# A hybrid attention block: where the attention's blocks are turned, and what stands in line ahead of what in the gates and at SwiGLU's end

## The chip, the cores and the metric

The kernel runs on one core of a Trainium2 chip. Its five engines (TensorE or PE for matmuls, VectorE or DVE, ScalarE or ACT, GpSimd or POOL, and SyncE or SP, which here only issues transfers) each work through a queue of their own in order and wait for one another by semaphores. The metric is the device time of one execution in microseconds (us), as a median of runs.

## What is computed

One residual layer over 512 tokens and 16 learned meta tokens of width 1024. Both attentions, their projections, the gates and SwiGLU are computed in fp32 to full precision; cut to what matters:

```python
xn = rmsnorm(h, norm_mix_g)
proj = xn @ w_in                                  # sq, sk, sv of 8 heads; dq, dk (two maps each), dv of 8 heads
# A: stick-breaking, blocks of 128 queries
z = q @ k.T * 128 ** -0.5                         # kpos < qpos
u = log_sigmoid(-z)
a = exp(log_sigmoid(z) + reverse_cumsum(u) - u)
o_sb = a @ v
# B: differential
p = softmax(q_c @ k_c.T / 8 - slope * dist)       # c = 0, 1; whole chunks of 64 ahead are seen
o_df = (p[0] - lam * p[1]) @ v                    # then a norm per head
gates = sigmoid(xn @ w_gate + b_gate)             # 2 x 1024
merged = gates[0] * (o_sb @ w_br_sb) + gates[1] * (o_df @ w_br_df)
h = h + merged @ w_out
hn = rmsnorm(h, norm_ffn_g)
h = h + (silu(hn @ w_ffn_gate) * (hn @ w_ffn_up)) @ w_ffn_down
y = rmsnorm(h, norm_final_g)[meta dropped]
```

## The kernel before

**Products.** Every fp32 product is made of three matmuls on numbers cut into a high part (`h`) and a rest (`l`): `mm3` (L291) issues high x high (L294), high x rest (L295) and rest x high (L296). The cut of a tile is two instructions in `split` (L77): ACT copies the high part (L78), DVE subtracts it for the rest (L79). Weights pass in chunks of 512 KB through SP's queue (L208) into `wst`, and `generic` (L220) splits each into `wh` and `wl` a few chunks ahead of its use.

**Order.** A planner orders each engine's queue at build time from program order, dependences, priorities (`tc.high_priority(offset=EVAC)` pulls evacuations forward) and its own model of time. So an instruction can stand in a queue ahead of one that comes before it in the program. `behind(ins, name)` (L81) adds a dependence on an instruction kept in `cast`, so that `ins` comes after it.

**Attention.** Eight stick-breaking heads (`sb_head`, L614), then eight differential ones (`df_head`, L698). While a head's scores are made into probabilities by ACT and DVE, PE runs projections of the next head and other "units" in the places where the head's generator yields a number (L1038). `attn_out` (L548) turns a head's probabilities so that PE can multiply them with v: ten blocks of 128 x 128, by PE transposes (L559, L561) into PSUM. Row j = 0 of blocks has four, j = 1 three, j = 2 two, and one diagonal block is kept plain. `turn_first` turns j = 0 and 1 (seven blocks) into two banks, each followed by its evacuation into `a_h` (ACT, L563) and `a_l` (DVE, L564), and makes the small edge blocks `a_s` by DVE's own transposes (L572). One unit of PE work later `turn_rest` turns the other three and copies `a_f` (ACT, L578). One more unit later `weighted` (L580) multiplies: three groups of `mm3`, then `a_f` and `a_s` (L586, L587).

PSUM has eight banks: two `z` tiles of two banks each (`z_tile`) and four `mm` tiles of one bank (`mm_tile`; `tr_tile` is the same pool). The stick-breaking head turns j = 0 and 1 into the first banks of two `z` tiles and the other three blocks into the second bank of the first of them. The differential head uses three `mm` tiles. `weighted` takes a `z` tile in both.

**Gates.** The loop over `merge_order` (L1115) goes through the eight column blocks f in the order 1, 2, 0, 3, ... 7. For both branches it loads y from DRAM (SP, L1069), takes the gate (from the unit, or for f = 0 from DRAM, L1121) and multiplies: on POOL for f < 6 (L1127), on DVE for 6 and 7 (L1129). DVE adds the two (L1133), for f = 3 to 6 behind the last weight split. `merge_sums` splits the result for the output product. Loads of x into `hres` on POOL's queue are placed behind the last POOL product (L1142).

**SwiGLU.** Gate and up products are made in seven products a block pair (a Strassen-like scheme in 256-token halves): `first`, `second`, `third` for each of the 22 column blocks f. In `second` (L1321) ACT copies `qx` out of bank e1 after product s2, so that s3 can write there, and `qy` after s3; DVE adds e3 to `qy`. In `third` (L1335) product a22 goes to e1 and makes `aT[:, f, T1]`, then s4 goes to e3 and makes `aT[:, f, T2]` by a silu. For f = 21, the last, no `first(f + 1)` stands between `second` and `third`. The down products follow; `act_parts` (L1366) splits their activations (`da`: ACT L1374, DVE L1375), and the planner may place those and the first down weights early.

Of the kernel before, what the change touches and what calls it, by code (L numbers as in the profile page):

```python
# [9 lines left out]
F32 = mybir.dt.float32  # L10
# [31 lines left out]
def block_kernel(ctx: ExitStack, tc: tile.TileContext, x, meta, norm_mix_g, w_in, w_gate, b_gate,  # L42
# [33 lines left out]

    def split(hi, lo, src, lo_eng=None, hi_copy=None):  # L77
        cast["last"] = (hi_copy or nc.scalar.copy)(hi, src)  # L78
        cast["lo"] = (lo_eng or nc.vector).tensor_tensor(lo, src, hi.bitcast(F32), op=ALU.subtract)  # L79

# [139 lines left out]
    def generic(n):  # L220
        wh, wl = parts(n)
        split(wh, wl, staged[n], nc.gpsimd if n < 3 else None)
        cast["split"] = cast["lo"]
# [323 lines left out]

    def attn_out(blocks, d, lo_rows, banks):  # L548

# [5 lines left out]

        def turn(j, pt):
            n = 512 - j * P
            for t in range(j, NQ):
                nc.tensor.transpose(pt[:, (t - j) * P:(t - j + 1) * P], blocks(t, j * P, (j + 1) * P), ident)  # L559
            if j == 2:  # L560
                nc.tensor.transpose(pt[:, 384:512], blocks(3, 3 * P, 4 * P), ident)  # L561
            c = slice(off[j], off[j] + n)
            nc.scalar.copy(a_h[:, c], pt[:, 0:n])  # L563
            nc.vector.tensor_tensor(a_l[:, c], pt[:, 0:n], a_h[:, c].bitcast(F32), op=ALU.subtract)  # L564

        def turn_first():
            for j, pt in enumerate(banks(2)):
                turn(j, pt)
            for t in range(NQ):
                b = blocks(t, (t + 1) * P - 32 + NM, (t + 1) * P + NM)  # L570
                for i in range(qn // 32):
                    nc.vector.transpose(a_s[32 * t:32 * t + 32, t * qn + 32 * i:t * qn + 32 * i + 32],  # L572
                                        b[lo_rows + 32 * i:lo_rows + 32 * i + 32])

        def turn_rest():
            p2 = banks(1)[0]
            turn(2, p2)
            nc.scalar.copy(a_f, p2[:, 384:512])  # L578

# [10 lines left out]

        return turn_first, turn_rest, weighted

# [21 lines left out]
    def sb_head(h, d, o_h, o_l):  # L614
# [29 lines left out]
        base = ((0, 0), (0, 144), (0, 416), (1, 0))  # L644
        zs = []

        def banks(n):
            if n == 1:
                return [zs[0][:, 1]]
            zs.extend((z_tile(), z_tile()))  # L650
            return [z[:, 0] for z in zs]

        t1, t2, av = attn_out(lambda t, k0, k1: res[base[t][0]][:, base[t][1] + k0:base[t][1] + k1], d, 96, banks)
        yield 4 if h + 1 < SEVEN else 5
        t1()
        yield 1
        t2()
        yield 1
        ps = av()
# [38 lines left out]
    def df_head(h, d, o_h, o_l):  # L698
# [55 lines left out]
        maps(3)  # L754
        t1, t2, av = attn_out(lambda t, k0, k1: prs[t][:, 0, k0:k1], d, 64, lambda n: [tr_tile() for _ in range(n)])
        yield 3 if h < NH - 1 else 2
        t1()
        yield 1
        t2()
        yield 1  # L760
        ps = av()
# [353 lines left out]
    for i, f in enumerate(merge_order):  # L1115
# [3 lines left out]
        for br, y in enumerate(ys[i]):  # L1119
            if f == 0:  # L1120
                nc.sync.dma_start(sg[br], g_part[br])  # L1121
                nc.scalar.activation(sg[br], sg[br], AF.Sigmoid)
            elif f > 2:
                for u in gate(br, f, sg[br], AF.Sigmoid):
                    u()
            if f < 6:
                cast["gated"] = nc.gpsimd.tensor_tensor(sg[br], sg[br], y, op=ALU.mult)  # L1127
            else:
                nc.vector.tensor_tensor(sg[br], sg[br], y, op=ALU.mult)  # L1129
        if f == KT - 1:  # L1130
            prepare(prep_at["out", "s1", 2])
        m = mf[:, f] if f < 4 else sg[0]
        merged = nc.vector.tensor_tensor(m, sg[0], sg[1], op=ALU.add)  # L1133
        if 2 < f < KT - 1:
            behind(merged, "split")
# [144 lines left out]
    with tc.tile_pool(name="ffn", bufs=1) as fp:  # L1280
# [40 lines left out]
        def second(f):  # L1321
# [3 lines left out]
            with tc.high_priority(offset=EVAC):  # L1325
                nc.scalar.copy(qx, e1)  # L1326
            ready(at_job(c3, f) + 2)
            product(f, "s1", tsum["t1"], e3, True)
            product(f, "s3", tsum["t3"], e1, False)
            with tc.high_priority(offset=EVAC):  # L1330
                nc.scalar.copy(qy, e1)
                nc.vector.tensor_tensor(qy, e3, qy, op=ALU.add)
            return qx, qy

        def third(f, qx, qy):  # L1335
            e1, e2, e3, sg = bank[f]
            product(f, "a22", tsum["t4"], e1, False)
            with tc.high_priority(offset=EVAC):
                nc.vector.scalar_tensor_tensor(aT[:, f, T1], e1, -1.0, sg[:, T1], op0=ALU.mult, op1=ALU.mult)
            product(f, "s4", tsum["b22"], e3, False)  # L1340
            with tc.high_priority(offset=EVAC):
                nc.vector.tensor_tensor(sg[:, T2], e3, qx, op=ALU.add)
            nc.scalar.activation(sg[:, T2], sg[:, T2], AF.Silu)
            nc.vector.scalar_tensor_tensor(aT[:, f, T2], qy, -1.0, sg[:, T2], op0=ALU.mult, op1=ALU.mult)

# [20 lines left out]
        def act_parts(upto):  # L1366

            for i in range(len(acts), min(len(order_of), upto)):
# [4 lines left out]
                src, sign = block(b, k0), -1.0 if b == "t2" else 1.0  # L1373
                nc.scalar.activation(a[:, 0, 0:n], src, AF.Copy, scale=sign)  # L1374
                nc.vector.scalar_tensor_tensor(a[:, 1, 0:n], src, sign, a[:, 0, 0:n].bitcast(F32), op0=ALU.mult, op1=ALU.subtract)  # L1375
# [163 lines left out]
```

## Time and profile before

| what | value |
|---|---|
| median of 3 runs | 944.86 us (944.44 to 946.46) |
| the profiled execution | 942.7 us |
| its span, first to last instruction | 940.9 us |
| PE busy | 925.6 us |
| DVE busy | 731.7 us |
| ACT busy | 582.3 us |
| POOL busy | 188.2 us |

The span is what the engines' records cover; the rest of the execution's time lies around it. A busy PE is not a PE at its peak: matmuls are pipelined, a record of 0.39 us is followed by the next one's start 0.23 us later, so the distance of the starts tells what a matmul costs, and a wait costs its idle time and some of the overlap. The views used are: the page; the waits (who waited for whom, in total, times, longest); windows (busy time and count of each engine in a stretch, then clock, DMA share, GB/s); and the timeline (start, duration, engine, line, operation, output<-inputs, shape, count, and in brackets the idle time before it and what ended it). Stages by the timeline: stick-breaking heads to about 225 us, differential heads to 490, gates to 560, output product and norm to 610, SwiGLU to 829, down product to the end.

### The profile page before, as it was taken

To read this page: it belongs to the slowest core of one execution; us is meant where nothing else is said; L and a number is where in the kernel's file an instruction comes from. 1 tells how busy PE (TensorE), PEld (TensorE's weight loads), DVE (VectorE), ACT (ScalarE), POOL (GpSimd) and SP (SyncE) were. 2 spreads that over 40 slices of the span, in tenths; PEclk is the share of its full clock that TensorE was granted. 3 is DMA by queue.
4 is the path that set the end of the run, shared out by engine and by line. 5 is a ranking of instruction groups with operands and counts; after the bars stand their busy time and mean duration, and the time that the engine had idled before them with its cause. 6 is when DMAs were issued, how large, how long until landed. Compare 5 with 4: busy or idle time off the path is not lost.

```text
span 940.9 us, 16049 instructions
## 1 busy us (share of the span) xinstructions
PE 925.6 (98%) x6010; PEld 842.0 (89%) x6010; DVE 731.7 (78%) x1400; ACT 582.3 (62%) x1102; POOL 188.2 (20%) x211
## 2 busy tenths in 40 slices
PE   8999999999999999999999999999999999999997
PEld 5988999898999899998988788899999999988886
DVE  7988877776677766877662678899888888999775
ACT  7665676676656666666754456765555555566554
POOL 4000121222333344343504440001000000000013
PEclk9999999999999999999999999999999999999999
DMA  8525778778777878799977775627753343286642
GB/s 250 152 62 157 174 175 198 166 168 250 190 194 175 219 173 190 172 194 200 195 184 190 191 260 165 168 73 165 156 131 105 101 125 90 68 267 202 198 150 90
DMA packets 155823, 158.41 MB, mean 168 GB/s; under 512 B 6465, under 2 KB 117218, under 8 KB 155746
## 3 DMA queue, kind: packets, MB, share of 16 engines
q1 hardware_dynamic: 132690, 101.61, 36.2%
q0 software_dynamic: 22896, 55.72, 28.7%
q8 instruction: 47, 0.77, 0.3%
q14 instruction: 30, 0.25, 0.1%
q10 hardware_dynamic: 160, 0.07, 0.0%
HBM read 133.64 MB, written 50.86 MB: 196 GB/s over the span
## 4 chain that ended last, share of the span: by engine, by line
PE 79%; DVE 11%; issue 3%; ACT 3%; DMA 1%; POOL 1%; SPq 0%; ACTq 0%; POOLq 0%; DVEq 0%
PE mm L295 18%; PE mm L296 18%; PE mm L294 18%; PE z L294 6%; PE z L296 6%; PE z L295 6%; DVE wl L79 3%; DVE s L640 2%; PE z L709 1%; PE z L708 1%; PE tr L559 1%; DVE s L641 1%; DVE s L636 1%; PE tr L535 1%; POOL y_df L804 1%
## 5 line engine op out<-in xcount | busy, mean ns | idle before, releaser
L295 PE MATMUL mm<-xT_l,wh 128*128 128x264 f32 (+2 forms) x656 | 213.6, 326 | 0.5
L294 PE MATMUL mm<-xT_h,wh 128*128 128x264 f32 (+2 forms) x656 | 213.6, 326 | 0.5 <-ACT xT_h L913 0.5
L296 PE MATMUL mm<-xT_h,wl 128*128 128x264 f32 (+2 forms) x656 | 212.7, 324 | 0.5 <-DVE wl L79 0.5
L79 DVE TENSOR_TENSOR wl<-wst,wh 128x1024 fp32r<-128x1024 f32 (+1 forms) x147 | 165.8, 1132 | 32.6 <-ACT wh L78 32.2
L78 ACT CAST wh<-wst 128x1024 fp32r<-128x1024 f32 (+1 forms) x147 | 141.8, 966 | 77.0 <-PE mm L295 56.2
L296 PEld LDWEIGHTS mm<-xT_h,wl 128*128 128x128 f32 x656 | 123.5, 188 | 10.9 <-DVE wl L79 0.9
L295 PEld LDWEIGHTS mm<-xT_l,wh 128*128 128x128 f32 x656 | 123.4, 188 | 10.3 <-DVE xT_l L914 1.3
L294 PEld LDWEIGHTS mm<-xT_h,wh 128*128 128x128 f32 x656 | 123.4, 188 | 9.9 <-ACT xT_h L913 0.9
L294 PE MATMUL mm<-hT_h,wh 128*128 128x256 f32 x304 | 85.8, 284 | 1.4 <-ACT qx L1326 0.8
L296 PE MATMUL mm<-hT_h,wl 128*128 128x256 f32 x304 | 85.9, 283 | 0.0
L295 PE MATMUL mm<-hT_l,wh 128*128 128x256 f32 x304 | 85.7, 283 | 0.0
L294 PEld LDWEIGHTS mm<-hT_h,wh 128*128 128x128 f32 x304 | 57.9, 191 | 2.0 <-ACT qx L1326 1.3
L296 PEld LDWEIGHTS mm<-hT_h,wl 128*128 128x128 f32 x304 | 58.0, 191 | 0.0
L295 PEld LDWEIGHTS mm<-hT_l,wh 128*128 128x128 f32 x304 | 58.0, 191 | 0.0
L712 DVE CUSTOM_DVE_ANT_0 pr<-z,bias 128x144 f32<-128x144 f32 (+3 forms) x64 | 30.9, 501 | 34.2 <-PE z L709 31.9
L294 PE MATMUL mm<-o_h,wh 128*128 128x512 f32 x128 | 53.0, 414 | 0.0
L1441 POOL TENSOR_TENSOR outs<-hres,gF 128x512 f32<-128x512 f32 x4 | 6.2, 1546 | 222.7 <-DVE hres L1427 216.0
L294 PE MATMUL z<-wh,da 128*128 128x512 f32 (+1 forms) x132 | 50.2, 381 | 0.0
L295 PE MATMUL z<-wl,da 128*128 128x512 f32 (+1 forms) x132 | 50.2, 381 | 0.0
L296 PE MATMUL z<-wh,da 128*128 128x512 f32 (+1 forms) x132 | 50.2, 380 | 0.0
L296 PE MATMUL mm<-o_h,wl 128*128 128x512 f32 x128 | 50.1, 391 | 0.0
L295 PE MATMUL mm<-o_l,wh 128*128 128x512 f32 x128 | 50.0, 390 | 0.0
(364 smaller groups left out, 2507.7 us busy)
## 6 DMA issues: line engine op xcount, KB each, us to landing
wst<-in_w_in_dram SPq DMA_DIRECT2D x40, 512.0 KB, 6.1
ds<-in_w_ffn_down_dram POOLq DMA_DIRECT2D x30, 512.0 KB, 6.0
wst<-in_w_ffn_gate_dram SPq DMA_DIRECT2D x22, 512.0 KB, 3.9
wsu<-in_w_ffn_up_dram SPq DMA_DIRECT2D x20, 512.0 KB, 4.0
wst<-in_w_gate_dram SPq DMA_DIRECT2D x16, 512.0 KB, 6.4
y_df<-y_out POOLq DMA_DIRECT2D x32, 256.0 KB, 7.8
slots<-ds SPq DMA_DIRECT2D x13, 512.0 KB, 3.3
os<-in_w_out_dram POOLq DMA_DIRECT2D x12, 512.0 KB, 4.6
```

Source lines behind the costliest of these rows:

```text
L78: cast["last"] = (hi_copy or nc.scalar.copy)(hi, src)
L79: cast["lo"] = (lo_eng or nc.vector).tensor_tensor(lo, src, hi.bitcast(F32), op=ALU.subtract)
L294: nc.tensor.matmul(ps, lhsT=ah, rhs=bh, start=(start and i == 0), stop=False, skip_group_check=skip)
L295: nc.tensor.matmul(ps, lhsT=ah, rhs=bl, start=False, stop=False, skip_group_check=skip)
L296: nc.tensor.matmul(ps, lhsT=al, rhs=bh, start=False, stop=(stop and i == n - 1), skip_group_check=skip)
L535: nc.tensor.transpose(pt[:, j * P:(j + 1) * P], vT[:, j * P:(j + 1) * P], ident)
L559: nc.tensor.transpose(pt[:, (t - j) * P:(t - j + 1) * P], blocks(t, j * P, (j + 1) * P), ident)
L636: nc.vector.scalar_tensor_tensor(s, zz, 0.0, e, op0=ALU.max, op1=ALU.add)
L640: nc.vector.tensor_tensor_scan(f, resets[:, L - (b - a):][:, ::-1], f, BIG, op0=ALU.mult, op1=ALU.add)
L641: nc.vector.tensor_tensor(s, zz, s, op=ALU.subtract)
L708: nc.tensor.matmul(o, lhsT=q[c][:, qs], rhs=k[c][:, 0, k0:k1], start=True, stop=False)
L712: nc.vector.tensor_tensor_reduce(po, zz, bb, scale=1.0, scalar=-3.0e38, op0=ALU.add, op1=ALU.max, accum_out=mx[:, t, c:c + 1])
```

## The change

Three edits. First, `attn_out` turns all ten blocks in one place, before any of their copies, into the four banks of two `z` tiles in both kinds of head (j = 0 and j = 2 in the banks of the first, j = 1 and the diagonal block in those of the second); the copies follow, then the edge blocks; two units then stand between this place and `weighted`. Second, the gate products of f < 6 go from POOL to DVE, and the merge of f = 0 also goes behind the last weight split. Third, at SwiGLU's end the first down weight's high part is cast behind `qy` of the last block, the first two activation parts behind its `qx`, and the last block's `third` makes its s4 half before its a22 half.

```diff
-    def split(hi, lo, src, lo_eng=None, hi_copy=None):
+    def split(hi, lo, src, lo_eng=None, hi_copy=None, after=None):
         cast["last"] = (hi_copy or nc.scalar.copy)(hi, src)
+        if after:
+            behind(cast["last"], after)
...
-        split(wh, wl, staged[n], nc.gpsimd if n < 3 else None)
+        split(wh, wl, staged[n], nc.gpsimd if n < 3 else None, after="qy" if n == first_down else None)
...
-        def turn(j, pt):
...
-        def turn_first():
...
+        def turned():
+            z0, z1 = z_tile(), z_tile()
+            banks = z0[:, 0], z1[:, 0], z0[:, 1]
+            for j, pt in enumerate(banks):
+                for t in range(j, NQ):
+                    nc.tensor.transpose(pt[:, (t - j) * P:(t - j + 1) * P], blocks(t, j * P, (j + 1) * P), ident)
+            nc.tensor.transpose(z1[:, 1, 0:P], blocks(3, 3 * P, 4 * P), ident)
+            for j, pt in enumerate(banks):
+                n = 512 - j * P
+                c = slice(off[j], off[j] + n)
+                nc.scalar.copy(a_h[:, c], pt[:, 0:n])
+                nc.vector.tensor_tensor(a_l[:, c], pt[:, 0:n], a_h[:, c].bitcast(F32), op=ALU.subtract)
+            nc.scalar.copy(a_f, z1[:, 1, 0:P])
             for t in range(NQ):
...
-        def turn_rest():
-            p2 = banks(1)[0]
-            turn(2, p2)
-            nc.scalar.copy(a_f, p2[:, 384:512])
...
-        t1()
-        yield 1
-        t2()
-        yield 1
+        turned()
+        yield 2
...
+            gated = nc.vector.tensor_tensor(sg[br], sg[br], y, op=ALU.mult)
             if f < 6:
-                cast["gated"] = nc.gpsimd.tensor_tensor(sg[br], sg[br], y, op=ALU.mult)
-            else:
-                nc.vector.tensor_tensor(sg[br], sg[br], y, op=ALU.mult)
+                cast["gated"] = gated
...
-        if 2 < f < KT - 1:
+        if f not in (1, 2, KT - 1):
             behind(merged, "split")
...
-                nc.scalar.copy(qx, e1)
+                cast["qx"] = nc.scalar.copy(qx, e1)
...
-                nc.scalar.copy(qy, e1)
+                cast["qy"] = nc.scalar.copy(qy, e1)
...
+            for half in (up, gate_and_up) if f < NFF - 1 else (gate_and_up, up):
+                half()
...
-                nc.scalar.activation(a[:, 0, 0:n], src, AF.Copy, scale=sign)
+                part_h = nc.scalar.activation(a[:, 0, 0:n], src, AF.Copy, scale=sign)
+                if i < 2:
+                    behind(part_h, "qx")
```

`up` holds the a22 half and `gate_and_up` the s4 half of `third`, each with its evacuations as before.

More of the change, by code (lines that the diff above doesn't have):

```diff
@@ L546, in v_units, with attn_out @@
         return kv_units(key, lambda ps, s: nc.scalar.copy(vT[:, s], ps)), turn
-    def attn_out(blocks, d, lo_rows, banks):
+    def attn_out(blocks, d, lo_rows):
         qn = P - lo_rows
@@ L554, in attn_out @@
         a_f = ap_.tile([P, P], F32, tag="a_f", name="a_f")
-        def turn(j, pt):
[L557 to L564, printed above, removed]
-        def turn_first():
-            for j, pt in enumerate(banks(2)):
-                turn(j, pt)
+        def turned():
[11 more added lines that the diff above has]
+            nc.scalar.copy(a_f, z1[:, 1, 0:P])
             for t in range(NQ):
@@ L589, in weighted @@
             return ps
-        return turn_first, turn_rest, weighted
+        return turned, weighted
     def sb_units(h):
@@ L644, in sb_head @@
         base = ((0, 0), (0, 144), (0, 416), (1, 0))
[L645 to L653, printed above, removed]
+        turned, av = attn_out(lambda t, k0, k1: res[base[t][0]][:, base[t][1] + k0:base[t][1] + k1], d, 96)
         yield 4 if h + 1 < SEVEN else 5
-        t1()
-        yield 1
-        t2()
-        yield 1
+        turned()
+        yield 2
         ps = av()
@@ L754, in df_head @@
         maps(3)
-        t1, t2, av = attn_out(lambda t, k0, k1: prs[t][:, 0, k0:k1], d, 64, lambda n: [tr_tile() for _ in range(n)])
+        turned, av = attn_out(lambda t, k0, k1: prs[t][:, 0, k0:k1], d, 64)
         yield 3 if h < NH - 1 else 2
[L757 to L760, printed above, removed]
+        turned()
+        yield 2
         ps = av()
@@ L1336, in third, with up, gate_and_up @@
             e1, e2, e3, sg = bank[f]
[L1337 to L1344, printed above, removed]
+            def up():
+                product(f, "a22", tsum["t4"], e1, False)
+                with tc.high_priority(offset=EVAC):
+                    nc.vector.scalar_tensor_tensor(aT[:, f, T1], e1, -1.0, sg[:, T1], op0=ALU.mult, op1=ALU.mult)
+            def gate_and_up():
+                product(f, "s4", tsum["b22"], e3, False)
+                with tc.high_priority(offset=EVAC):
+                    nc.vector.tensor_tensor(sg[:, T2], e3, qx, op=ALU.add)
+                nc.scalar.activation(sg[:, T2], sg[:, T2], AF.Silu)
+                nc.vector.scalar_tensor_tensor(aT[:, f, T2], qy, -1.0, sg[:, T2], op0=ALU.mult, op1=ALU.mult)
+            for half in (up, gate_and_up) if f < NFF - 1 else (gate_and_up, up):
+                half()
         for f in range(2):
```

## The prediction

> **What bounds the kernel now.** I read the page first, then PE's waits, then short windows around each stall, then the timeline of those places.
>
> ```profile
> span 940.9 us, 16049 instructions
> ...
> PE 925.6 (98%) x6010; PEld 842.0 (89%) x6010; DVE 731.7 (78%) x1400; ACT 582.3 (62%) x1102; POOL 188.2 (20%) x211
> ```
>
> TensorE is the bound: 15.3 us of the span are not PE. No edit here removes a matmul or a transposed block, so all that can be won is PE's idle time and what a restart costs. The longest wait by cause, and the windows around the first six stick-breaking heads:
>
> ```profile
> PE z L559 <- DVE a_l L564: 1.8, 2, 1.0
> ...
> 48.00:57.00 9.00, 8.01 (x67) 7.75 (x66) 8.89 (x18) 4.46 (x10) 0.00 (x0) 1.00 0.01 2
> 79.00:87.00 8.00, 7.88 (x52) 6.98 (x51) 7.93 (x15) 5.46 (x10) 1.30 (x2) 1.00 0.71 205
> ...
> 161.00:170.00 9.00, 8.17 (x53) 7.29 (x52) 8.90 (x17) 6.78 (x12) 1.69 (x3) 1.00 0.69 196
> 188.00:197.00 9.00, 8.89 (x56) 7.84 (x55) 8.91 (x17) 6.62 (x12) 2.28 (x3) 1.00 0.76 220
> ```
>
> First column behind the window: its length, then PE's busy time. PE is idle 0.99 us in the first, 0.83 in the fifth, and about 0.12 in the other four (the first and the last of them are shown): 2.3 together. DVE is nearly full in each (8.89 of 9.00). So in these heads PE waits for a DVE that is behind.
>
> **Part 1, the ten blocks.** Now the blocks of a head are turned as 7 and, one unit of matmuls later, 3. The late three go into the second bank of the tile whose first bank is still being read:
>
> ```profile
> 82.76 1.15 DVE L564 TENSOR_TENSOR a_l<-z,a_h 128x512 fp32r<-128x512 f32 x2
> ...
> 83.49 0.44 PE L559 MATMUL z<-ident,s 128*128 128x128 f32 x2
> ...
> 85.63 0.42 DVE L564 TENSOR_TENSOR a_l<-z,a_h 128x256 fp32r<-128x256 f32 x1
> ...
> 86.62 0.40 PE L294 MATMUL z<-a_h,vh 128*128 128x512 f32 x1
> ```
>
> The first a_l of the pair ends at about 83.37 (0.6 us of the 1.15), and the late blocks start 0.12 behind it. After the change the three are issued before any copy reads the tiles, so this wait cannot be there. What it costs is more than the idle time, as a head with the wait and one without it show:
>
> ```profile
> 188.92 0.93 PE L559 MATMUL z<-ident,s 128*128 128x128 f32 x7
> ...
> 195.99 0.40 PE L294 MATMUL z<-a_h,vh 128*128 128x512 f32 x1
> ...
> 216.07 0.93 PE L559 MATMUL z<-ident,s 128*128 128x128 f32 x7
> ...
> 222.84 0.40 PE L294 MATMUL z<-a_h,vh 128*128 128x512 f32 x1
> ...
> 224.85 0.60 PE L535 MATMUL tr<-ident,vT 128*128 128x128 f32 x4
> ...
> 225.28 0.27 PE L542 MATMUL tr<-ident,v_s 128*128 128x128 f32 x1
> ```
>
> From the first block to the weighted sum: 7.07 us with the wait, 6.77 without, for the same work; 0.30 for 0.11 idle, so a restart costs about 0.19. Over six heads: 2.3 + 6 x 0.19 = 3.4 us lost. A block itself takes 0.11 (four in 0.43), in one group or in two: moving three is free.
>
> What is late next? The weighted sum needs the third a_l, now 85.63 to 86.05. It goes to right behind the pair, about 84.3, with PE wanting it at 86.3: two us of room. Head 0 has less:
>
> ```profile
> 54.75 0.55 DVE L564 TENSOR_TENSOR a_l<-z,a_h 128x384 fp32r<-128x384 f32 x1
> ...
> 56.70 0.40 PE L294 MATMUL z<-a_h,vh 128*128 128x512 f32 x1
> ```
>
> Without the 1.15 us of its stall PE gets there at 55.55, while the second a_l ends at 55.30 and the third at about 55.7; up to 0.3 of the stall may remain. DVE's and ACT's work queued behind (weight halves, kl, vT) moves back by the third copy, 0.4 us, and no wait for those shows in these windows. I take **2.9 of the 3.4 us**; bounds 0 (DVE's lateness turns up at the next wait) and 3.4.
>
> In the eight differential heads the blocks move from mm tiles to z tiles:
>
> ```profile
> 276.14 0.93 PE L559 MATMUL tr<-ident,pr 128*128 128x128 f32 x7
> ...
> 278.55 1.16 DVE L564 TENSOR_TENSOR a_l<-tr,a_h 128x512 fp32r<-128x512 f32 x2
> ...
> 280.44 0.48 PE L294 MATMUL z<-a_h,vh 128*128 128x512 f32 x1
> ```
>
> There is no idle time to win. There is a new wait: the weighted sum's own z tile is one of the two just used, so it starts only when the copies out of that one are done. The pair of a_l ends at 279.71; the third (0.42) would end near 280.1, 0.3 before PE's 280.44. I take **nothing**; bounds 0 and the rival below.
>
> The clock is 1.00 in every window above, those with seven blocks in a row among them, so ten should not change it. The Trainium skill (TensorE: Matmul & The Clock Gate, Part 4: PE-mode transpose) says that transposes do not count as PE activity in the way matmuls do, which speaks against longer runs of them. By that rule the granted clock could fall behind each group; the windows do not bear it out, and it is a rival below.
>
> **Part 2, the gates.** Twelve gate products go from POOL to DVE, and the merge of f=0 is queued behind the last weight split.
>
> ```profile
> 527.35 1.30 POOL L1127 TENSOR_TENSOR sg<-sg,y_df 128x512 f32<-128x512 f32 x1 [0.71 <-ACT sg L1122]
> ...
> 528.68 0.69 DVE L1133 TENSOR_TENSOR mf<-sg 128x512 f32<-128x512 f32 x1 [1.76 <-POOL sg L1127]
> 529.29 2.31 DVE L79 TENSOR_TENSOR wl<-wst,wh 128x1024 fp32r<-128x1024 f32 x1
> ...
> 530.55 0.39 PE L294 MATMUL mm<-xT_h,wh 128*128 128x512 f32 x1
> 530.78 0.39 PE L295 MATMUL mm<-xT_l,wh 128*128 128x512 f32 x1
> 531.66 0.50 PE L296 MATMUL mm<-xT_h,wl 128*128 128x512 f32 x1 [0.49 <-DVE wl L79]
> ...
> 559.16 0.69 DVE L1129 TENSOR_TENSOR sg<-sg,y_sb 128x512 f32<-128x512 f32 x1
> ```
>
> DVE stood at f=0's merge 1.76 us for POOL's product; the weight half behind it, 2.31 us where the same form takes 1.22 (826.16 below), came too late. PE steps 0.88 there where its step is 0.23 (530.55 to 530.78), and I add 0.11 for the restart, the smaller of those seen here: 0.76 lost. After the change the half goes first and a product costs DVE 0.69 in place of POOL's 1.30. The twelve add 12 x 0.69 = 8.3 us to a DVE that stands waiting in this stage; the products of f=6 and 7 are already done so. In the other queues: SP's loads of the next y stand behind the products and come 0.6 earlier each; POOL's last three y_df accumulations are no longer behind a waiting product; the hres loads start earlier. I take **0.75**; bounds 0.76 and a loss where a product waiting for its y holds up weight halves behind it (a rival).
>
> **Part 3, the end of SwiGLU.** In f=21 ACT's copy qx comes behind the first down weight's cast:
>
> ```profile
> 821.61 0.63 ACT L1374 ACTIVATE da<-aT 128x512 fp32r<-128x512 f32 x1 [0.81 <-DVE wl L79]
> 822.15 1.04 ACT L78 CAST wh<-wst 128x1024 fp32r<-128x1024 f32 x1
> ...
> 822.67 0.28 PE L295 MATMUL z<-t_l,wh 128*128 128x256 f32 x1
> 822.78 0.28 PE L296 MATMUL z<-t_h,wl 128*128 128x256 f32 x1
> 823.81 0.39 PE L294 MATMUL mm<-hT_h,wh 128*128 128x256 f32 x1 [0.75 <-ACT qx L1326]
> 824.04 0.28 PE L295 MATMUL mm<-hT_l,wh 128*128 128x256 f32 x1
> ...
> 825.54 0.37 ACT L1331 COPY qy<-mm 128x256 f32<-128x256 f32 x1 [0.83 <-PE mm L296]
> 826.04 0.31 PE L294 MATMUL mm<-t_h,wh 128*128 128x256 f32 x1
> ...
> 826.16 1.22 DVE L79 TENSOR_TENSOR wl<-wst,wh 128x1024 fp32r<-128x1024 f32 x1
> 827.30 0.42 DVE L1332 TENSOR_TENSOR qy<-z,qy 128x256 f32<-128x256 f32 x1
> ...
> 827.77 0.39 PE L294 MATMUL z<-hT_h,wh 128*128 128x256 f32 x1
> ```
>
> PE steps 1.03 to the row at 823.81 where 0.11 is due, and 0.23 from it where 0.12 is: 1.03. The row at 827.77 waited for the sum qy, which stood behind the 1.22 us half until 827.64: 12 matmuls from 826.04 at 0.12 would have ended at 827.48, so 0.29, and a restart of 0.11. Together 1.4. With the cast (1.04) behind qy, qx can go at 822.15 and PE does not wait. But the cast also fed three down matmuls (3 x 0.23 = 0.69) that filled the time until qy was copied; now nothing fills it. If a22 goes first it waits for ACT's copy alone, as now: 0.7 lost. If s4 does, as the code now says, it waits for the copy and for DVE's add (about 0.42) too: 1.1, and 1.2 more if a weight half stands in front. Net: 1.4 - 0.7 = 0.7 to 1.4 - 1.1 = 0.3, and -0.9 at worst. I take **0.5**.
>
> **The sum.** 2.9 + 0.75 + 0.5 = 4.15. The profiled execution took 942.7 with its span of 940.9, so 938.5; the median of the runs shown is 944.86, 2.2 above it, and I subtract from that: **940.7 us**.
>
> **Rivals.** *(a) The lateness moves on* (0.24): DVE is full in the first six heads, so the weighted sum, the weight halves or the next scores wait instead, and only part comes back: half of Part 1, all of Part 2, nothing of Part 3 is 1.45 + 0.75 = 2.2, and less if more moves: 943 or so. For it: 8.9 of 9.0 us busy; against: two us of room at the next wait. *(b) The z tiles in the differential heads, slower* (0.06): if DVE takes one more weight half (1.22) before the third a_l, this ends 0.9 behind PE's arrival, and each of eight heads pays 0.9 + 0.12 + 0.19 = 1.2: 9.7 lost against 4.15, about 950. It decides from the moment at which that a_l ends later than 0.12 before the weighted sum; 0.3 says it does not. *(c) The gates on DVE* (0.07): a product that waits for its y stands ahead of a weight half. POOL now carries such waits; one misplaced costs PE what is left, from 1 to some 5 us; 941 to 946. *(d) The clock* (0.01): half speed for the 24 matmuls of 0.12 behind each group is 2.9 us for each of 16 heads, 46 in all: 987. That the late blocks still wait, so that the change doesn't do what it says, I count in (a). The **forecast**, 3 to 6 us off, gets 0.62.
>
> **Range and chances.** All bounds at their best, 3.4 + 0.76 + 1.4 and 0.3 for what I set at nothing, is 5.9: 939.0, and 938.6 with the scatter of a median. Upward it takes in (a) and the better half of (c): 944.4. About 0.2% (1.9 us) is what a measurement of this kernel can tell from no change. Faster by more: the forecast's 0.62 and half of (a), 0.74; slower by more: (b), (d) and part of (c), 0.10; the rest 0.16.
>
> **What would show it.** Right: no wait of L559 for a_l, windows of the first six heads full, ten blocks in one row of 1.3 us; DVE rows for the gate product and no POOL rows there, no PE wait for wl near 528; in f=21 qx directly behind the da row, and one wait of 0.7 to 1.1 at qy. Wrong: PE waits at the weighted sum (a_l or a_f) in either kind of head; PE's idle time moving to weight halves; DVE standing at a gate product with a half behind it.

## The result and the profile after

The kernel after takes 939.42 us (median of 7 runs, 937.64 to 941.17). The kernel before, run beside it, takes 944.86 (7 runs, 942.80 to 946.55). The ratio is 0.9941, with a 95% interval of 0.9925 to 0.9957: faster by 0.4 to 0.75%, 5.4 us by the medians. The profiled executions are 942.7 and 938.57 us, 4.1 apart. The forecast was 940.7 in a range of 938.6 to 944.4.

The page and the waits of TensorE of the kernel after (the diff has moved the lines: the blocks are L563 and L564, `a_h` and `a_l` L568 and L569, `mm3` L296 to L298, the cut's rest L81):

```profile
span 936.8 us, 16027 instructions
...
PE 924.1 (99%) x6009; PEld 842.4 (90%) x6010; DVE 734.3 (78%) x1412; ACT 583.5 (62%) x1102; POOL 168.3 (18%) x199
```

```profile
...
PE z L893 <- DVE xs L888: 1.2, 2, 0.7
PE mm L296 <- ACT hT_h L1157: 1.1, 1, 1.1
...
PE mm L296 <- ACT qy L1315: 0.5, 1, 0.5
PE mm L296 <- ACT qq L451: 0.2, 1, 0.2
PE mm L296 <- ACT qx L1310: 0.2, 1, 0.2
```

The blocks' wait for `a_l`, the wait for `wl` and the wait of 0.75 us for `qx` are gone. New are `qy` (0.46), `qq` (0.25) and a short one for `qx` in f = 20 (0.19), and the wait for `hT_h`, which was 0.55, is 1.08. The windows around the heads:

```profile
48.00:57.00 9.00, 9.00 (x72) 8.66 (x71) 8.90 (x19) 5.24 (x12) 0.00 (x0) 1.00 0.01 2
79.00:87.00 8.00, 8.00 (x54) 7.37 (x53) 7.48 (x12) 4.74 (x10) 1.30 (x2) 1.00 0.62 181
...
161.00:170.00 9.00, 9.00 (x57) 8.12 (x57) 8.98 (x14) 5.90 (x13) 2.52 (x3) 1.00 0.67 178
...
```

PE is full in all six of them, at a clock of 1.00. A stick-breaking and a differential head in the timeline:

```profile
78.26 1.14 PE L563 MATMUL z<-ident,s 128*128 128x128 f32 x9
79.25 0.27 PE L564 MATMUL z<-ident,s 128*128 128x128 f32 x1
...
84.33 0.41 DVE L569 TENSOR_TENSOR a_l<-z,a_h 128x256 fp32r<-128x256 f32 x1
...
85.01 0.40 PE L296 MATMUL z<-a_h,vh 128*128 128x512 f32 x1
...
275.33 1.58 DVE L569 TENSOR_TENSOR a_l<-z,a_h 128x512 fp32r<-128x512 f32 x3
...
277.23 0.48 PE L296 MATMUL z<-a_h,vh 128*128 128x512 f32 x1
```

Ten blocks in 1.26 us (1.14 and the row of one, from 78.26 to 79.52), then 6.75 from the first block to the weighted sum (85.01). In the differential head the third `a_l` ends at 276.91, 0.32 ahead of the sum.

Where the time went is read from the start of the same matmul in both timelines: how much earlier it comes in the kernel after.

| at | before | after | earlier by | gained since the row above |
|---|---|---|---|---|
| first block of x behind PE's longer wait for `xs` | 10.16 | 9.88 | 0.28 | 0.28 |
| weighted sum of the seventh stick-breaking head | 222.84 | 219.67 | 3.17 | 2.89 |
| turn in the seventh differential head | 457.51 | 454.34 | 3.17 | 0.00 |
| last differential head's end | 490.64 | 487.24 | 3.40 | 0.23 |
| gates, behind the wait for `wl` | 532.94 | 528.73 | 4.21 | 0.81 |
| SwiGLU's first product that waits for `hT_h` | 607.23 | 603.52 | 3.71 | -0.50 |
| first s1 matmul of f = 21 | 821.54 | 817.93 | 3.61 | -0.10 |
| second group of the down product | 829.31 | 825.01 | 4.30 | 0.69 |
| end of the span | 940.9 | 936.8 | 4.1 | -0.2 |

The first row is not the change's doing: `xs` is x as it is loaded at the start, and PE's longer wait for it was 1.13 us before and 0.70 after.

### The profile page after: what moved, and what is told of

Same layout as the page of the kernel before. It is cut to its first block, busy times and chain, and to the rows that moved or that the text cites. A ratio compares the mean times of both kernels' runs of the same rounds, so it can differ in the third digit from the quotient of the medians.

```text
span 936.8 us, 16027 instructions
## 1 busy us (share of the span) xinstructions
PE 924.1 (99%) x6009; PEld 842.4 (90%) x6010; DVE 734.3 (78%) x1412; ACT 583.5 (62%) x1102; POOL 168.3 (18%) x199
## 4 chain that ended last, share of the span: by engine, by line
PE 91%; DVE 4%; ACT 2%; DMA 2%; issue 1%; SPq 0%; ACTq 0%; DVEq 0%
PE mm L296 22%; PE mm L297 21%; PE mm L298 21%; PE z L296 6%; PE z L298 6%; PE z L297 6%; PE z L563 2%; PE z L696 1%; PE z L695 1%; DVE wl L81 1%; PE tr L537 1%; ACT wh L78 1%; DMA lam<-in_lam_k_dram 1%; DMA wsu<-in_w_ffn_up_dram 1%; PE z L584 1%
## 5 line engine op out<-in xcount | busy, mean ns | idle before, releaser
L296 PE MATMUL mm<-xT_h,wh 128*128 128x264 f32 (+2 forms) x656 | 213.6, 326 | 0.5 <-ACT xT_h L898 0.5
L298 PE MATMUL mm<-xT_h,wl 128*128 128x264 f32 (+2 forms) x656 | 212.5, 324 | 0.0
L81 DVE TENSOR_TENSOR wl<-wst,wh 128x1024 fp32r<-128x1024 f32 (+1 forms) x147 | 163.0, 1113 | 30.9 <-ACT wh L78 30.5
L296 PEld LDWEIGHTS mm<-xT_h,wh 128*128 128x128 f32 x656 | 123.4, 188 | 10.0 <-ACT xT_h L898 0.9
L298 PEld LDWEIGHTS mm<-xT_h,wl 128*128 128x128 f32 x656 | 123.4, 188 | 9.9
L296 PE MATMUL mm<-hT_h,wh 128*128 128x256 f32 x304 | 85.7, 283 | 1.3 <-ACT hT_h L1157 1.1
L298 PE MATMUL mm<-hT_h,wl 128*128 128x256 f32 x304 | 85.9, 283 | 0.0
L296 PEld LDWEIGHTS mm<-hT_h,wh 128*128 128x128 f32 x304 | 57.9, 191 | 1.7 <-ACT hT_h L1157 1.3
L298 PEld LDWEIGHTS mm<-hT_h,wl 128*128 128x128 f32 x304 | 58.0, 191 | 0.0
L296 PE MATMUL mm<-o_h,wh 128*128 128x512 f32 x128 | 52.4, 410 | 0.0
L296 PE MATMUL z<-wh,da 128*128 128x512 f32 (+1 forms) x132 | 50.3, 381 | 0.0
L298 PE MATMUL z<-wh,da 128*128 128x512 f32 (+1 forms) x132 | 50.2, 380 | 0.0
L298 PE MATMUL mm<-o_h,wl 128*128 128x512 f32 x128 | 50.1, 391 | 0.0
L151 POOL DMA_DIRECT2D ds<-in_w_ffn_down_dram x36 | 30.1, 840 | 91.8 <-ACT wh L78 62.2
```

The lines of the kernel that those rows point to most:

```text
L151: tc.add_manual_dep(nc.gpsimd.dma_start(dst, src, **kw).ins, cast["last"].ins.name, paced)
L296: nc.tensor.matmul(ps, lhsT=ah, rhs=bh, start=(start and i == 0), stop=False, skip_group_check=skip)
L298: nc.tensor.matmul(ps, lhsT=al, rhs=bh, start=False, stop=(stop and i == n - 1), skip_group_check=skip)
```

## The experiments

**The first edit alone.** The kernel before with `attn_out`, `sb_head` and `df_head` as in the first part of the diff above, and nothing else.

> The kernel before with the ten blocks in one place and nothing else. Theory S (the late three blocks wait because they write into a tile whose other bank is still being read): no wait of a block for a_l is left, the first six stick-breaking heads take 7.07 - 0.30 = 6.77 us from the first block to the weighted sum, and the span falls by 2.6 to 3.2 us, a ratio of 0.9966 to 0.9973. Theory L (PE waits because DVE is behind, whatever it waits for): PE waits at the weighted sum instead, and less than 1.5 us comes back.

Measured: 941.75 us (940.62 to 942.28), ratio to before 0.9970 (0.9959 to 0.9981), so 2.8 us by it, with 1.8 to 3.9 in the interval. No block waits for `a_l`, and from the first block to the weighted sum five of the six heads take 6.74 or 6.75 us and the first 7.06, as theory S has it. So by the times the first edit brings about half of the 5.4 us. Its one profile shows less, a span of 939.8 us, 1.1 below before's. From the first block of the first head to the weighted sum of the seventh 2.1 us are gained: PE waits 0.47 us for `qq` near 150 us, and in the fifth head 0.20 for the third `a_l` at the weighted sum, so a little of theory L is there. Later the gates' wait (0.56) and the one for `qx` in f = 21 (0.75) stand as before, and PE waits 0.99 for `qx` in f = 20 too, of which more below.

**The late blocks in a tile of their own.** The late three blocks of the kernel before go to an `mm` tile; the place is as before.

```diff
             if n == 1:
-                return [zs[0][:, 1]]
+                return [tr_tile()]
```

> The kernel before with one word changed: in the stick-breaking heads the late three blocks go to an mm tile of their own, still one unit behind the seven. Theory S: the blocks no longer wait although they come as late as before, and 2.3 to 3.4 us come back, about as much as from one place. Theory P (it is the one place that matters, since a late block waits for late copies wherever it goes): the wait for a_l stays, and under 0.5 us comes back.

Measured: 943.67 (941.72 to 945.77), ratio 0.9991 (0.9979 to 1.0002). Its waits of PE:

```profile
PE mm L294 <- ACT qx L1326: 0.9, 2, 0.7
PE z L295 <- DVE a_l L564: 0.9, 1, 0.9
PE mm L294 <- DVE ql L604: 0.6, 1, 0.6
```

No block waits any more though they come as late as before, so theory P is out: the late blocks waited because their bank belongs to the tile that was being read. Nothing read that bank itself. The Trainium skill (PSUM — Partial Sum Buffer, section "PSUM bank collisions raise a hardware error") asks for a guard by bank and quadrant, or more simply by bank; by that rule the two banks of a `z` tile would need none between them. But two waits come in place of it. In the first head the third `a_l`, still made late, holds up the weighted sum (L295, 0.85 us at 58.45), and in the fifth an `mm` tile is missing (0.62 at 165.91). Between the same matmuls, at 52.15 and 193.16 us of before's timeline, 0.95 us are gained, not 2.3 to 3.4, and the times can't be told from those of before. Turning all ten in one place does two things, then: it takes the wait away, and it brings the third copy forward.

**The gates.** Three runs: both halves of that edit, then each by itself, all on the kernel before. The halves:

```diff
-        if 2 < f < KT - 1:
+        if f not in (1, 2, KT - 1):
             behind(merged, "split")
```

```diff
+            gated = nc.vector.tensor_tensor(sg[br], sg[br], y, op=ALU.mult)
             if f < 6:
-                cast["gated"] = nc.gpsimd.tensor_tensor(sg[br], sg[br], y, op=ALU.mult)
-            else:
-                nc.vector.tensor_tensor(sg[br], sg[br], y, op=ALU.mult)
+                cast["gated"] = gated
```

> The kernel before with the twelve products on DVE and the merge of f=0 behind the split, nothing else. PE's step of 0.88 us in front of the weight half near 531 us becomes 0.23 and no wait of PE for wl is listed; PE is 0.7 to 0.85 us earlier behind the gates than in front of them. If DVE's new products hold up weight halves, a new PE wait for wl of 0.3 us or more shows between 510 and 560.

> The kernel before with one half of the edit in the gates: the merge of f = 0 goes behind the last weight split, the products stay on POOL. Theory O (the wait is one of order: DVE stood at the merge for POOL's product with the weight half behind it): the wait of PE for wl near 531 us is gone, its step there is 0.23 in place of 0.88 us, though the half still takes up to 2.31 us beside POOL's products; 0.6 to 0.8 us gained up to 535 us. Theory P (it is one of speed: the products must leave POOL): the half still shares its time with POOL, and PE still waits 0.3 us or more for it. Behind 535 us nothing changes by either.

> The kernel before with the other half of the edit in the gates: the products go to DVE, the merge of f = 0 keeps its place ahead of the weight half. Theory P (speed): a product from 527.35 takes 0.69 in place of 1.30 us, the merge 0.69, the half 1.22 in place of 2.31, so the half ends near 530.0, over 1 us ahead of PE's use at 531.2; the wait is gone, 0.6 to 0.8 us gained. Theory O (order): the merge still makes the half wait for its product, and a wait of PE of 0.3 us or more stays near 531 us. If both halves of the edit take the wait away alone, either would have done, and the other adds nothing.

Measured, one run each: 942.82 with both, 943.88 with the order alone, 944.61 with the products on DVE alone. Times of single runs can't be told apart here; the traces can. With both halves PE has no wait for `wl`, and between 248 and 533 us it gains 0.81 us on before (0.74 behind to 0.07 ahead); with the products on DVE alone there is no wait either, and it gains 0.75 (1.91 behind to 1.16). With the order alone a wait of 0.18 stays. But the queues of the program with the order alone came out the same as before's on every engine, instruction by instruction, and those of the program with both the same as with the products alone. So the order edit does nothing in these four programs: the queues already met it, and 0.18 and 0.49 are two draws of one program. (No run has the kernel after without it.) It is the products on DVE that matter. POOL's and SP's queues and ACT in the kernel before:

```profile
499.03 3.57 POOL L1127 TENSOR_TENSOR sg<-sg,y_sb 128x512 f32<-128x512 f32 x2 [23.85 <-DMA y_sb<-y_sb]
502.55 4.41 POOL L804 DMA_DIRECT2D y_df<-y_out  x5
515.34 1.28 POOL L1127 TENSOR_TENSOR sg<-sg,y_df 128x512 f32<-128x512 f32 x1 [8.38 <-DMA y_df<-y_df]
...
519.65 0.42 SPq L1121 DMA_DIRECT2D sg<-g  x1
...
526.64 0.63 ACT L1122 ACTIVATE sg<-sg 128x512 f32<-128x512 f32 x1 [1.08 <-POOL sg L1127]
```

and what answers to it in the kernel after, with the merge of f = 0 and the weight half behind it:

```profile
496.95 0.86 POOL L789 DMA_DIRECT2D y_df<-y_out  x1 [24.91 <-ACT y_out L785]
...
505.10 0.86 POOL L789 DMA_DIRECT2D y_df<-y_out  x1 [0.49 <-ACT y_out L785]
...
512.41 0.69 DVE L1111 TENSOR_TENSOR sg<-sg,y_df 128x512 f32<-128x512 f32 x1 [10.18 <-DMA y_df<-y_df]
...
514.83 0.42 SPq L1106 DMA_DIRECT2D sg<-g  x1
...
519.83 0.63 ACT L1107 ACTIVATE sg<-sg 128x512 f32<-128x512 f32 x1 [1.43 <-DMA sg<-g]
...
521.22 0.69 DVE L1117 TENSOR_TENSOR mf<-sg 128x512 f32<-128x512 f32 x1
521.83 1.22 DVE L81 TENSOR_TENSOR wl<-wst,wh 128x1024 fp32r<-128x1024 f32 x1
```

Before, the issues of the y_df sums (L804) stood behind a product on POOL; five went out together from 502.55 on. After, they go out one by one from 496.95 on. That is not what brings the merge of f = 0 forward. Measured from PE's end of the heads (490.64 and 487.24, the table's row), the fifth sum is issued at the same point, 15.3 and 15.1 us behind it, and the first product that needs y back from DRAM starts 24.70 and 25.17 us behind it. The time is won behind that product. From it to SP's second load of the gate of f = 0 pass 4.31 us before and 2.42 after: two products and two merges lie between, and the products take 1.28 and 1.61 us on POOL, with another sum between them, and 0.69 and 0.68 on DVE. From the issue of that load to ACT's sigmoid pass 6.99 and 5.00 us (in before the load landed at 526.56, just as the product named in the bracket ended); why the load is shorter is not shown. From the sigmoid to the merge, with the last product, pass 2.04 and 1.39. So the merge comes at 521.22 in place of 528.68, 7.46 us earlier, of which 3.40 is PE's lead, and the half behind it takes 1.22 in place of 2.31 beside a POOL product.

The other profiles agree. In the nine with the products on DVE the half starts 33.9 to 36.2 us behind the heads' end and takes 1.22, in the five with them on POOL 38.4 to 40.0 and 2.30 to 2.32, while the first y_df product comes at 24.3 to 25.7 and at 23.7 to 26.1. Theory P, the speed of the products, was the nearer one. In the profile of before the shorter half alone would have been enough, by an estimate from its rows: 529.29 + 1.22 = 530.51, where PE wanted it at 531.01.

**SwiGLU's end alone.** The third part of the diff on the kernel before.

> The kernel before with the third edit alone (the cast behind qy, two activation parts behind qx, the last block's halves the other way round). The step of 1.03 us for qx goes; a wait of 0.6 to 0.8 us for qy takes the place of the three down matmuls; from the start of f=21 to the middle of the down products PE gains 0.3 to 0.7 us. If the add of qy stands behind a weight half, the new wait is 1.1 to 2.3 us and nothing is gained.

Measured: one run of 947.06. At its own place it does what it should: from the first s1 matmul of f = 21 to the second group of the down product 7.08 us (825.40 to 832.49) where before has 7.77 (821.54 to 829.31), the wait for `qx` gone and one of 0.46 for `qy` in its place. The run as a whole took longer than before, mostly for a reason in the untouched gates (0.8 us more went in the fifth head's wait for `a_l` and 1.2 in the down product, at waits for `hres`). Its timeline in the gates:

```profile
503.51 4.43 POOL L806 DMA_DIRECT2D y_df<-y_out  x5
517.68 1.28 POOL L1129 TENSOR_TENSOR sg<-sg,y_df 128x512 f32<-128x512 f32 x1 [9.74 <-DMA y_df<-y_df]
...
533.92 0.50 PE L298 MATMUL mm<-xT_h,wl 128*128 128x512 f32 x1 [1.79 <-DVE wl L81]
...
535.40 0.63 PE L296 MATMUL mm<-xT_h,wh 128*128 128x512 f32 x1
535.83 0.63 PE L297 MATMUL mm<-xT_l,wh 128*128 128x512 f32 x1
```

and its window, busy PE 8.21 and clock 0.83:

```profile
530.00:540.00 10.00, 8.21 (x30) 6.28 (x29) 6.37 (x8) 3.83 (x7) 4.29 (x3) 0.83 0.55 139
```

Here the transfer came 14.2 us behind the sums (503.51 to 517.68), in the profile of before 12.8, and PE waited 1.79 us in place of 0.49. Then seven matmuls stepped 0.43 in place of 0.23. That wait costs 1.94 more than a step, 0.11 behind it and about 1.6 at the lower clock: 3.6 us, where the profile of before shows 0.76.

The third edit also shortens a wait that the profile of before does not list. The run with the order alone, whose queues are those of before, has it in f = 20, the block ahead of the last:

```profile
805.75 0.69 DVE L238 TENSOR_TENSOR s<-wsu 128x512 f32<-128x512 f32 x1 [2.31 <-DMA wsu<-in_w_ffn_up_dram]
...
812.67 0.63 ACT L1374 ACTIVATE da<-aT 128x512 fp32r<-128x512 f32 x1 [0.37 <-DVE wl L79]
813.20 0.60 ACT L78 CAST wh<-wst 128x512 fp32r<-128x512 f32 x1
813.71 0.36 ACT L1326 COPY qx<-mm 128x256 f32<-128x256 f32 x1
...
814.13 0.39 PE L294 MATMUL mm<-hT_h,wh 128*128 128x256 f32 x1 [0.93 <-ACT qx L1326]
```

and the kernel after, where DVE had waited 2.42 us for the same load:

```profile
809.34 0.38 PE L296 MATMUL mm<-hT_h,wh 128*128 128x256 f32 x1 [0.19 <-ACT qx L1310]
```

The copy `qx` stands behind an activation part `da`, which waits for a weight half on DVE, which is late when the load of an up weight (`wsu`) is. In the six profiles without the third edit PE is idle there for 0.11 us (before), 0.18, 0.40, 0.93, 0.94 and 0.99, where DVE had waited 1.49, 1.58, 1.80, 2.31, 2.34 and 2.39 us for the load. With the edit no `da` stands ahead of this copy any more, and in eight profiles PE is idle 0.20 us at most, four of them with a wait of DVE of 2.2 to 2.4 us.

**What is left of the wait at `qy`.** Two runs on the kernel after: the a22 half first again, and the first down weight's cast behind `qx`, so that down matmuls can fill the wait as they did before.

```diff
-            for half in (up, gate_and_up) if f < NFF - 1 else (gate_and_up, up):
+            for half in (up, gate_and_up):
```

```diff
-        split(..., after="qy" if n == first_down else None)
+        split(..., after="qx" if n == first_down else None)
```

> The kernel after, with the a22 half of the last block ahead of its s4 half again. After, PE stands 0.46 us for the copy qy (step 0.74 where 0.12 is due), and the row that waits is the first of a22, since the queue starts with six matmuls of a22 in spite of the text's order. Theory Q (the wait is for the copy out of the bank that a22 writes, and the order of the halves in the text changes nothing): the same wait of 0.4 to 0.5 us at the same place, and from it to the middle of the down product within 0.2 us of after. Rival (s4 first is what keeps it so short, or what makes the last silu early enough): the wait grows by 0.3 to 0.7 us or another appears at the first use of the last block's aT.

> The kernel after, with the first down weight's cast behind the last qx in place of the last qy, so that three down matmuls can fill PE's wait for the copy of qy as they did before the change. Theory Q (that cover is what the change gave up, 0.62 us beside 0.12): if the weight's two halves are ready in time the wait of 0.46 us for qy goes and 0.4 to 0.6 us are gained. Rival R (the halves are not: the cast of 1.04 us stands ahead of the copy qy on ACT, and the weight's rest of 1.22 us ends behind that): qy is copied up to 1.0 us later, PE waits for wl or for qy, and 0.5 to 1.2 us are lost. I hold R for likelier, because after qx ACT has da copies and then this cast ahead of qy.

The end of SwiGLU in the kernel after, to read them against:

```profile
818.13 0.37 ACT L1310 COPY qx<-mm 128x256 f32<-128x256 f32 x1 [0.23 <-PE mm L298]
818.53 2.19 ACT L1364 ACTIVATE da<-aT 128x512 fp32r<-128x512 f32 x4
...
820.91 0.37 ACT L1315 COPY qy<-mm 128x256 f32<-128x256 f32 x1 [0.18 <-PE mm L298]
821.31 2.00 ACT L78 CAST wh<-wst 128x1024 fp32r<-128x1024 f32 x2
821.33 0.39 PE L296 MATMUL mm<-t_h,wh 128*128 128x256 f32 x1 [0.46 <-ACT qy L1315]
```

Measured: 940.14 and 938.75, one run each. With a22 first the wait is 0.46 again, and the stretch from s1 to the second down group is 7.00 us where after has 7.08 (817.93 to 825.01): the order of the halves is worth nothing, as the copy is what is waited for. With the cast at `qx` the wait for `qy` goes, one of 0.33 for `wh` comes, and the stretch is 6.93: 0.15 gained, where I held 0.5 to 1.2 lost for likelier. One down matmul of 0.23 is all the cover that fits.

**The norm ahead of SwiGLU.** PE's wait for `hT_h` grew from 0.55 to 1.08 us in a place that the change does not touch:

```profile
602.05 1.05 ACT L78 CAST wh<-wst 128x1024 fp32r<-128x1024 f32 x1 [1.41 <-DMA wst<-in_w_ffn_up_dram]
...
603.00 0.83 ACT L1157 ACTIVATE hT_h<-z,pcol 128x256 fp32r<-128x256 f32 x2
...
603.52 0.39 PE L296 MATMUL mm<-hT_h,wh 128*128 128x256 f32 x1 [1.08 <-ACT hT_h L1157]
```

The copies stand behind a cast that waits for its weight's transfer: 1.41 us here, 0.88 in before (at 605.75), 1.22, 1.23 and 0.74 in three other profiles with the whole change. The run turns the sixteen blocks of a half ahead of all copies:

```diff
             for i in range(2):
                 for t in range(2):
                     nc.tensor.transpose(pt[:, (2 * i + t) * P:(2 * i + t + 1) * P],
                                         hn[:, 2 * tp_ + t, (k + i) * P:(k + i + 1) * P], ident)
+        for k in range(0, KT, 2):
+            pt = banks[k // 2 % 2][:, k // 4]
             for i in range(2):
                 g = g_ffn[:, k + i:k + i + 1]
```

It ran beside the kernel after itself, and beside a version with the cast at `qx` as well.

> The kernel after, with the lesson of its first edit used once more: in the norm ahead of SwiGLU the sixteen blocks of a half are turned in one place ahead of the copies, in place of four at a time with the copies between. After, the second eight of the first half stand behind the copies out of the other bank of their tiles, and PE waits 1.08 us for hT_h at 603.5. Theory B (two banks of one tile count as one thing here too): no row of L1152 stands behind a copy, the wait for hT_h falls to below 0.4 us, and 0.8 to 1.4 us are gained against after on the same chip, 0.08 to 0.15%. Rival D (ACT's cast that waits 1.41 us for its weight's transfer sets the time): the copies out still stand behind that cast, PE's wait stays at 0.8 us or more or moves to the first projections, and the time is that of after within 0.4 us. A third way: turning sixteen needs both z tiles earlier, while the output product still uses them, and PE waits there: slower by up to 1 us.

> The kernel after once more, unchanged, to set the two others against on the same chip: 939 to 940.5 us, ratio to before 0.993 to 0.9955, with the wait for hT_h at 0.8 to 1.1 us, the wait for the copy qy at 0.46 us, and no wait of a turned block for a_l or of a matmul for wl in the gates.

> The version that could beat both: the sixteen blocks of the norm in one place, and the first down weight's cast behind the last qx (in the run with the cast alone, 6.94 us from the first s1 matmul of the last block to the second group of the down product, 7.08 after). Theory B: 0.9 to 1.5 us faster than after, ratio to before 0.9925 to 0.994 with after's ratio near 0.9945. Rival D: within 0.4 us of after.

Measured: 938.70 (938.31 to 939.42) for the norm, 938.46 (938.05 to 939.13) with the cast too, 939.99 (937.35 to 940.57) for the kernel after. Ratios to before: 0.9934 (0.9918 to 0.9950), 0.9931 (0.9915 to 0.9947), 0.9943 (0.9923 to 0.9963). The wait for `hT_h` is gone in the first and 0.2 in the second; it was 0.4 in this profile of the kernel after, where I expected 0.8 to 1.1. In the first run the two copies now stand ahead of the cast in ACT's queue (603.22, the cast at 604.30), so the cast's transfer no longer holds them. Medians are 1.3 and 1.5 us lower, but the intervals overlap and the kernel after has the fastest single run: likely faster, not shown by these times alone. The spread of the kernel after, 3.2 us, asks for a cause of its own.

**The transfer of lam.** Two of the profiles of these three runs have a wait of PE for `qq` near 150 us of over 1.5 us; the first profile of the kernel after has 0.25. Rows of the first:

```profile
139.65 0.29 DVE L826 TENSOR_TENSOR lp<-lam 128x128 f32<-128x128 f32 x1 [1.22 <-DMA lam<-in_lam_k_dram]
...
149.31 0.39 PE L296 MATMUL mm<-tA,wh 128*128 128x264 f32 x1 [0.25 <-ACT qq L451]
```

and of the same kernel's second profile:

```profile
141.32 0.29 DVE L826 TENSOR_TENSOR lp<-lam 128x128 f32<-128x128 f32 x1 [2.48 <-DMA lam<-in_lam_k_dram]
...
142.98 0.20 ACT L829 ACTIVATE ls<-ls 128x2 f32<-128x2 f32 x1 [3.11 <-DVE ls L828]
...
150.52 0.41 ACT L451 COPY qq<-mm 128x264 f32<-128x264 f32 x1
150.98 0.39 PE L296 MATMUL mm<-tA,wh 128*128 128x264 f32 x1 [1.52 <-ACT qq L451]
```

DVE waits for four small loads, ACT waits for DVE with `o_h` and later `qq` queued behind, and PE gets what exceeds about 1 us. The last run, on the best version so far, sends these loads far ahead into a tile of their own.

```diff
-        lam4 = opool.tile([P, 4, 64], F32, tag="sg1", name="lam4")
-        for i, v in enumerate((lam_q1, lam_k1, lam_q2, lam_k2)):
-            nc.sync.dma_start(lam4[:, i], v.broadcast_to([P, 64]))
...
+    lam4 = ap_.tile([P, 4, 64], F32, tag="lam4", name="lam4", bufs=1)
+
+    def lam_loads():
+        for i, v in enumerate((lam_q1, lam_k1, lam_q2, lam_k2)):
+            nc.sync.dma_start(lam4[:, i], v.broadcast_to([P, 64]))
...
+            if (br, h) == (0, 3):
+                lam_loads()
```

> The run of the norm's blocks and the cast, with the four small loads of lam in a tile of their own and queued far ahead of their use. In seven profiles with the ten blocks in one place DVE waits for the last of these loads at the product lp, and PE waits for ACT's copy qq some 9 us later: 0.41 us on DVE goes with none on PE, 1.22 with 0.25, 1.46 with 0.49, 1.48 with 0.52, 2.48 with 1.52 and 2.65 with 1.61. Theory L (DVE's wait for lam is the cause: it holds the next o_h, vh and qq copies on ACT, and PE gets what is over about 1 us of it): no wait at lp, no wait of PE for qq near 150 us, the steps there as in the run with 0.41; 0.5 to 0.7 us less than the run without this edit (938.46 median), 937.4 to 938.2, with its runs within 1 us of one another. Rival C (the qq wait comes from the late weight sum ahead of it, and lam only fills the time): PE's wait for qq stays at 0.25 us or more, and the time within 0.3 us. Rival S: the loads go out in the first 30 us of the kernel and hold up the weights behind them on SP's queue: up to 1 us lost in the first head.

Measured: 937.01 (936.39 to 937.51), ratio to before 0.9913 (0.9891 to 0.9935). At that place:

```profile
148.40 0.38 ACT L451 COPY qq<-mm 128x264 f32<-128x264 f32 x1
...
149.26 0.29 PE L296 MATMUL mm<-tA,wh 128*128 128x264 f32 x1
```

No wait at `lp`, and none of PE for `qq`. The loads went out at 10.67 to 16.04 us, ahead of weights on SP's queue; in the first head this run is 0.19 us behind the one without the edit, as it was at 21 us already. This is theory L. The median is 1.4 us below 938.46, against 0.5 to 0.7 expected, but not all of that is shown to be lam's: the two ran on different chips beside different runs of before, and their intervals overlap. In the two profiles PE gains 0.77 us at this place, and 0.83 more near 870 us, in the down product, where the run without the edit waits for sums into `hres` and this one doesn't. By the medians and intervals it beats the kernel before by 0.65 to 1.1%; against the kernel after, its slowest run (937.51) stands 0.2 above the fastest of that kernel's thirteen (937.35) and below the other twelve, and both were run beside different runs of before.

## Why the prediction came out as it did

**Part 1** was forecast at 2.9 and the heads bring 2.89, which is luck in part: the blocks gave more than I took, and a wait that I had not seen took 0.5 back. From first block to weighted sum the six heads now take 7.05 and five times 6.75; before they took 8.11, 7.06, 7.08, 7.08, 7.80 and 7.06. That is 3.39 of the 3.4 that I set as the bound. Head 0 kept 0.3 over the others, as feared. What was "late next" is where the step failed: I looked for it at the weighted sum, the weight halves and `vT`, and it was `qq`, 0.41 us over its step and 0.11 behind it. The cause was no DVE that is full but the transfer of lam: in the profile of before it cost nothing at `lp`, and PE came later. Rival (a), lateness that moves on, has this much truth, with the 0.20 for the third `a_l` in the run with the blocks alone; the price was not half of the part but 0.5 us, and up to 1.6 of idle time in other executions. In the differential heads nothing was won or lost in seven, and the third `a_l` is 0.32 early against 0.3 forecast. Rival (b) fell. The last of them gave 0.23 that I had not priced.

**Part 2**: 0.75 forecast, 0.81 in the profiles. The symptom was read rightly: DVE stood at the merge of f = 0 with the half behind it. One step was wrong: "the half goes first". It doesn't; the merge edit leaves the queues as they were. The merge itself comes 4.06 us earlier against PE, since the products ahead of it are shorter on DVE and the gate's loads behind them go out earlier and land sooner, and the half no longer runs beside a POOL product. The prices that I named (0.69 for 1.30, 1.22 for 2.31) are what the rows show; "POOL's last three y_df accumulations" come earlier too, but y_df is not back any earlier. Rival (c) fell: DVE waits 10.18 us for y_df at 512.41 with weight halves behind it, and no PE wait for a half follows.

**Part 3**: 1.4 less 0.7 to 1.1, taken as 0.5; measured 0.69. The loss was at the smaller end: 0.62 over the step and 0.10 behind it, the 0.7 of "if a22 goes first". I followed the text's order (s4 first), and the planner queued six matmuls of a22 ahead. One reading is off: DVE's `qy` ended at 827.72 by its row, not at 827.64; nothing hangs on it. What the edit does in f = 20 I had not seen.

**Not seen**: 0.5 lost in front of SwiGLU, the growth of the wait for `hT_h`. The transfer behind it was issued 4.23 us earlier, with the rest (597.45 for 601.68), but the cast could start 4.60 us later in place of 4.07. In the second profile of the kernel after the wait is 0.42, in two more with the whole change 0.9: the term varies from execution to execution, and how much of it the change adds stays open.

**The sum**: 4.15 forecast, 4.1 between the profiled executions, but 5.4 between the medians. That the first two agree is luck in part: the three parts measure 2.89 + 0.81 + 0.69 = 4.39, and the table's other rows, the start, the last differential head, the norm and two waits in SwiGLU and the down product, cancel to -0.3. The step that was mis-sized is the last one: I took the sum of one execution off a median that lay 2.2 us above it, as if these 2.2 were no business of the change. Part of them is. The gates' wait, which the change removes, was 0.49 in the profile of before and 0.18, 0.40, 0.56 and 1.79 in four other profiles with those gates, and the last cost 3.6 us with its lower clock. The wait in f = 20, which it keeps at 0.20 or less, was 0.11 in before, the least of six, and up to 0.99 in the others. The fifth head's wait for `a_l` was 0.83 in before and 0.20, 0.80, 1.59 and 1.67 in four other profiles with those heads. That this makes up the 1.3 is likely but not shown, since the runs behind the medians have no profile; with the blocks alone the ratio gave 2.8 (1.8 to 3.9), so Parts 2 and 3 together look worth more by the medians than 1.25, within wide intervals.

**Rival (d)** fell: the clock is 1.00 in the windows with ten blocks in a row. The rule of the Trainium skill that I weighed there (TensorE: Matmul & The Clock Gate, Part 4: PE-mode transpose) costs nothing here, in runs of 1.3 us.

## What to carry to other kernels

A tile of several banks was one thing to this planner: write all of it, then read all of it, or give each its own tile. When a wait follows a transfer, its length in one profile is one draw: look at it in several before taking its price, and look there for waits that the first profile doesn't show. When work moves to another engine, measure the whole chain from one fixed point of PE's work, since what merely starts earlier is easily taken for the cause. And small loads that nothing hurries for are best queued long before their use: DVE, ACT and PE all stood behind four of them here.

## What the runs showed of the chip that I had not expected

An idle time of 1.79 us of PE was followed by seven steps of 0.43 us in place of 0.23 (clock 0.83 in those 10 us); idle times of 1.52 and 1.61 us at `qq` in two other runs were followed by full speed (clock 1.00 from 151 to 155 us), and so was one of 1.67 us for `a_l` at 166 us in the run with both halves of the gates' edit. The Trainium skill (TensorE: Matmul & The Clock Gate, section "Why this matters for your kernels") warns of gaps above some 3 us; here the clock fell behind a shorter one, once. The same small loads of lam let DVE wait from nothing to 2.65 us in thirteen profiles of nearly the same program up to there.
